# Attention in a hybrid decoder layer: the combination of a head in four later pieces, q regrouped on chip, weight loads one unit ahead of their splits

## The chip, the core and the metric

The kernel runs on one core of a Trainium2 chip. The core has a matrix engine (TensorE, PE in the profile; its weight loads are listed as PEld) and three engines for element-wise work: VectorE (DVE), ScalarE (ACT) and GpSimd (POOL). SyncE (SP) issues nearly all DMAs. Each engine takes its instructions in a fixed order; an instruction that waits holds up all that stand behind it. Matmul results lie in PSUM, all else on chip in SBUF.

The metric is the time of one execution in device microseconds: the median of several runs. A profiled execution gives a trace of every instruction; its times are for finding out where time goes.

## The reference

One decoder layer on a sequence of 2048 rows of 1024 numbers, in float32. What the change touches is the attention part: eight heads of 64 columns, and for each head three "branches", in which a query looks at keys at stride 1, 4 or 16. The branches are then combined by their softmax denominators.

```python
DILATED_BRANCHES = ((128, 1), (512, 4), (2048, 16))      # (window, dilation)

h = rms_norm(x)
z = h @ W_in                # columns: [conv u | gate B | gate C | q | k | v]
yA = B * causal_dwconv3(C * u)

def dilated_mixture(q, k, v):
    for window, dil in DILATED_BRANCHES:
        # query t attends to keys t, t - dil, t - 2*dil, ... down to t - window
        o, lse = dilated_branch(q, k, v, window, dil)     # softmax in float32
    w = softmax(stack(lses), axis=0)
    return sum(w * stack(outs), axis=0)

mix = concat(rms_norm(yA), rms_norm(yB))
x = x + mix @ W_out
x = x + swiglu(rms_norm(x))
```

## The kernel before

All products are computed in float16 with operands split into a high and a low half, so a float32 product is two or three matmuls. A weight is read as float32 ("raw"), its largest magnitude is found (L96, a maximum on VectorE, ends in the tile `vm_a`), it is scaled by a power of two and split into halves by ScalarE (a cast) and VectorE or GpSimd (a subtraction).

The kernel has these stages, one after another in PE's order.

1. Normalisation of the input and a first slice of the convolution (0 to 104 us).
2. Projections of q, k and v (104 to 368 us). There are 16 units: four pairs of heads, and for each pair four blocks of 512 rows. `project` does one unit: 192 matmuls (L1194), evictions by ScalarE (L1210), squares, a tail of small operations on VectorE and GpSimd that normalises q and k (it begins with L1214 on ScalarE and L1224 on VectorE), and the stores. v goes to DRAM as `d_v` (L1221), the halves of q and k as `d_qk` (L1243), and the halves of q once more as `d_q16` in the order of stride 16, in eight small stores (L1246). Between units the loop calls weight work. `operands` prepares the next pair's weights (in units 1, 5 and 9); `spill_conv` and `spill_out` prepare convolution and output weights and store them as halves in DRAM (in units 3, 6, 7, 8, 10, 11 and 12). Each loads its raw weights and works on them in the same call.
3. A transition, in which PE has 24 steps of convolution matmuls ("fill", 14.2 us) while the first pair's operands arrive.
4. Attention (401 to 752 us): per head 8 groups of the branch at stride 4 (b = 1), 4 at stride 16 (b = 2) and 8 at stride 1 (b = 0), so 160 groups. A group goes through a chain: s matmuls on PE (L1448), the exponential on ScalarE (L1453, tile `sm`), a mask on GpSimd (`affine_select`, L1461, one or two a group), a cast on ScalarE (L1464, `et`), the low half on VectorE (L1465), and the av matmuls on PE (L1475). The av matmuls of a group are issued three groups later; in between PE does s of later groups and about two fill steps a group (convolution and output projection).
5. The rest of the output projection and the feed-forward part (752 to 2140 us).

The operands of a pair come by `load_pair`: transposed DMA loads (L199) of q (`qT`), of k's high and low halves (`ka`, `kb`) from `d_qk`, and of `q16` from `d_q16`. They are all requested at one point, in the middle of the pair before.

The result of a group is copied from PSUM into `u` (L1480, L1483). For b = 1 and b = 2 the rows are in strided order; at the branch's end they go to DRAM as `d_u` and come back in natural order as `r` (L1492 to L1497), and the load is issued right behind the store. At the end of b = 0 `combine` is called twice, for 8 blocks of 128 rows each: two additions on GpSimd (L1400, L1401), a minimum, a maximum, a reciprocal and a scaling on VectorE (L1403 to L1406, tile `bm`), a multiplication on GpSimd (L1408) and a store (L1411). The last head does this on VectorE.

The order on each engine is set by a scheduler from the order in which the program issues instructions; `issue_after` puts an instruction behind another one.

## Time and profile before

| | |
|---|---|
| median of three runs | 2133.38 us (2132.79 to 2140.19) |
| profiled execution | 2142.32 us |
| its span, first to last instruction | 2140.6 us |
| mean granted PE clock | 0.984 |
| projections, 104 to 368.2 us | PE busy 256.9 of 264.2 |
| transition, 368.2 to 401.05 us | PE busy 14.2 of 32.85 |
| attention, 401.05 to 752 us | PE busy 324.9 of 350.95 |
| the rest, 752 to 2140.6 us | PE busy 1361.5 of 1388.6 |

PE is busy for 95% of the span. A row of a timeline gives the start, the duration, the engine, the line in the program, the operation, its output and inputs, the shapes and the count; in square brackets stands how long the engine was idle before it and what ended that. A row of waits reads: who waited for what, us in total, how often, the longest. The granted clock is the share of full speed at which PE was allowed to run.

### The profile page before, as it was taken

To read this page: it belongs to the slowest core of one execution; us is meant where nothing else is said; L and a number is where in the kernel's file an instruction comes from. 1 tells how busy PE (TensorE), PEld (TensorE's weight loads), DVE (VectorE), ACT (ScalarE), POOL (GpSimd) and SP (SyncE) were. 2 spreads that over 40 slices of the span, in tenths; PEclk is the share of its full clock that TensorE was granted. 3 is DMA by queue.
4 is the path that set the end of the run, shared out by engine and by line. 5 is a ranking of instruction groups with operands and counts; after the bars stand their busy time and mean duration, and the time that the engine had idled before them with its cause. 6 is when DMAs were issued, how large, how long until landed. Compare 5 with 4: busy or idle time off the path is not lost.

```text
span 2140.6 us, 34957 instructions
## 1 busy us (share of the span) xinstructions
PE 2027.0 (95%) x13368; PEld 1126.0 (53%) x13368; DVE 1320.6 (62%) x2483; ACT 1012.5 (47%) x1780; POOL 760.4 (36%) x809
## 2 busy tenths in 40 slices
PE   4999999698999999989999999999999999999998
PEld 2499998365566644434444444444444444444443
DVE  7454453355666877886776767676767565555454
ACT  7446566465666665553443333333433344343341
POOL 0024546355665621212221212121221246555463
PEclk9999999899999999999999999999999999999999
DMA  9568976558758477897333223322322762341432
GB/s 247 143 154 199 221 188 195 131 137 192 156 139 238 110 205 235 241 302 189 113 113 103 85 98 108 104 89 99 104 92 91 267 250 64 118 138 55 148 138 81
DMA packets 487411, 325.44 MB, mean 152 GB/s; under 512 B 274625, under 2 KB 440513, under 8 KB 485057
## 3 DMA queue, kind: packets, MB, share of 16 engines
q1 hardware_dynamic: 469552, 299.96, 50.0%
q10 hardware_dynamic: 17680, 23.16, 3.0%
q8 instruction: 106, 1.74, 0.3%
q14 instruction: 73, 0.59, 0.1%
HBM read 157.96 MB, written 121.04 MB: 130 GB/s over the span
## 4 chain that ended last, share of the span: by engine, by line
PE 65%; DMA 9%; DVE 7%; ACT 6%; SPq 5%; issue 4%; POOL 2%; DVEq 0%; ACTq 0%; POOLq 0%
PE ps L812 33%; PE ps L945 15%; SPq L199 3%; PE mm L191 3%; PE mm L192 3%; PE mm L193 3%; PE s L1448 2%; PE cvx L1194 2%; PE mm L1194 2%; PE av L1475 2%; DVE vm_a L96 1%; DMA nx_x<-in_x_dram 1%; DMA wq<-d_a 1%; DMA x<-d_x 1%; POOL sm L1461 1%
## 5 line engine op out<-in xcount | busy, mean ns | idle before, releaser
L812 PEld LDWEIGHTS <-w 128*128 128x128 f16 x3696 | 362.3, 98 | 451.5 <-issue 16.3
L812 PE MATMUL ps<-b,w 128*128 128x512 f16 x2112 | 465.9, 381 | 11.3 <-ACT s L863 5.5
L945 PE MATMUL ps<-b,w 128*128 128x512 f16 x1848 | 399.7, 379 | 2.2 <-DVE x L953 0.9
L812 PE MATMUL ps<-hb,w 128*128 128x512 f16 x1584 | 347.1, 379 | 0.0
L945 PEld LDWEIGHTS <-w 128*128 128x128 f16 x1848 | 180.8, 98 | 220.9 <-issue 3.4
L1194 PEld LDWEIGHTS <-b 128*128 128x128 f16 x3072 | 255.0, 98 | 9.1 <-issue 8.8
L705 POOL TENSOR_TENSOR t<-wq 128x512 f32<-128x512 f32 (+1 forms) x46 | 59.8, 1299 | 407.3 <-issue 230.7
L1461 POOL TENSOR_SCALAR_AFFINE_SELECT sm<-sm 128x256 f32<-128x256 f32 (+2 forms) x288 | 136.3, 495 | 143.2 <-ACT sm L1453 137.9
L1465 DVE TENSOR_TENSOR et<-sm,et 128x512 f16<-128x512 f32 (+1 forms) x160 | 121.2, 762 | 99.6 <-ACT et L1464 98.0
L818 DVE TENSOR_TENSOR s<-ps,s 128x512 f32<-128x512 f32 x220 | 150.2, 683 | 37.1 <-PE ps L812 36.6
L952 POOL TENSOR_TENSOR x<-x,s 128x512 f32<-128x512 f32 x72 | 103.0, 1432 | 170.5 <-DVE s L966 133.3
L1194 PE MATMUL cvx<-w,b 128*128 128x192 f16 x1776 | 151.2, 246 | 3.3 <-ACT f L1210 2.2
L1453 ACT ACTIVATE sm<-s,bound,kap 128x512 f32<-128x512 f32 (+1 forms) x160 | 119.1, 749 | 63.7 <-PE s L1448 33.7
L953 DVE SCALAR_TENSOR_TENSOR x<-ps,a_u,x 128x512 f32<-128x512 f32 x96 | 71.8, 749 | 100.9 <-PE ps L945 74.0
L1464 ACT CAST et<-sm 128x512 f16<-128x512 f32 (+1 forms) x160 | 93.8, 589 | 71.3 <-POOL sm L1461 70.2
L191 PE MATMUL mm<-b,wq 128*128 128x512 f16 x320 | 125.7, 393 | 0.0
L192 PE MATMUL mm<-b,wq 128*128 128x512 f16 x320 | 125.7, 393 | 0.0
L193 PE MATMUL mm<-b,wq 128*128 128x512 f16 x320 | 125.6, 392 | 0.0
L1194 PE MATMUL mm<-w,b 128*128 128x192 f16 x1296 | 113.0, 248 | 4.3 <-ACT f L1210 4.3
L722 ACT CAST w<-t 128x512 f16<-128x512 f32 x88 | 53.9, 618 | 128.7 <-PE ps L812 92.6
L1475 PE MATMUL av<-v,et 128*128 128x65 f16 x1800 | 85.4, 195 | 26.1 <-DVE et L1465 13.6
L96 DVE TENSOR_REDUCE vm_a<-wq 128x1 f32<-128x2048 f32 (+2 forms) x32 | 77.3, 2417 | 42.3 <-DMA wq<-in_w_up_dram 21.3
(288 smaller groups left out, 3215.7 us busy)
## 6 DMA issues: line engine op xcount, KB each, us to landing
d_a<-a ACTq DMA_DIRECT2D x88, 256.0 KB, 2.0
d_wd<-w SPq DMA_DIRECT2D x77, 256.0 KB, 2.0
wq<-d_a SPq DMA_DIRECT2D x64, 256.0 KB, 4.2
b<-d_wd SPq DMA_DIRECT2D x14, 1024.0 KB, 6.0
wq<-in_w_in_dram SPq DMA_DIRECT2D x24, 512.0 KB, 6.4
d_qk<-qkhl SPq DMA_DIRECT2D x16, 768.0 KB, 3.7
d_h<-hl SPq DMA_DIRECT2D x24, 512.0 KB, 3.2
wq<-in_w_gate_dram SPq DMA_DIRECT2D x22, 512.0 KB, 4.8
```

What stands on the lines that cost most here:

```text
L191: self.pe = mm(ps, lhsT=lh(k), rhs=rh(k), start=k == ks[0], stop=False)
L192: mm(ps, lhsT=lh(k), rhs=rl(k), start=False, stop=False)
L193: mm(ps, lhsT=ll(k), rhs=rh(k), start=False, stop=k == ks[-1])
L812: nc.tensor.matmul(ps[self.BANK[n]], lhsT=w[:, x, k], rhs=b[:, y, k], start=first and k == 0 and q == 0, stop=k == 3 and q == 2, skip_grou ...
L818: nc.vector.tensor_tensor(t, x, y, op=ALU.add)
L945: nc.tensor.matmul(ps[self.BANK[n]], lhsT=L[n][:, x, f], rhs=B[n][:, f, y], start=first and f == 0 and q == 0, stop=f == n_f - 1 and q == ...
L952: nc.gpsimd.tensor_tensor(o, o, s_, op=ALU.add)
L1194: self.pe = nc.tensor.matmul(ps[:, 192 * t:192 * (t + 1)], lhsT=lh(x, k), rhs=w[:, y, k], start=start and t + k + q == 0, stop=stop and k ...
L1453: nc.scalar.activation(e, sp[:, 0:o], AF.Exp, scale=self.kap, bias=self.bound)
L1461: nc.gpsimd.affine_select(m, m, pattern=pattern, compare_op=ALU.is_ge, fill=0.0, base=0, channel_multiplier=-sg)
L1465: nc.vector.tensor_tensor(et[:, 1], e, et[:, 0], op=ALU.subtract)
L1475: self.pe_av = nc.tensor.matmul(ps[:, us.index(u)], lhsT=p_, rhs=v_, start=n_ == 0, stop=n_ == len(ops) - 1)
```

## The change

1. `d_q16`, its stores and its transposed loads are gone. `regroup` makes `q16` of one head from `qT` on chip, by four copies on VectorE of 512 elements a partition, each 16 runs of 32 elements read with a step of 16. The first pair's first head is regrouped in unit 14 of the projections; in attention a pair's second head is regrouped at the pair's group 9, the next pair's first head at group 33. In the order that results, the first pair's eight copies all stand in the projections, the other 24 in attention.
2. `load_pair` is a generator. The first pair's twelve transposes are requested in units 8 to 11; of later pairs one is requested every second group. The loads of v are issued before the branch that needs them.
3. The load of `r` is issued two groups after its store. `combine` stops before its multiplication, and its four parts (additions and small operations, then multiplication and store, for each half) are called four, five, six and seven groups after the head's last output, each placed behind that group's mask.
4. `sm` has four buffers instead of three.
5. `operands`, `spill_conv` and `spill_out` are generators too: the raw loads are issued in one unit, the maximum, scaling and split in the next. The splits stand in units 1 to 10.

```diff
-        self.d_q16 = [dr.tile([S, 2 * P], F16, name=f"d_q16{g}") for g in range(4)]
...
-            for g in range(4):
-                Wg = Wn
-                for i in range(4):
-                    with ExitStack() as behind:
...
-                        if g < 3 and i == 1:
-                            Wn = self.operands(g + 1)
...
-                        k = self.SPILLS.get((g, i))
-                        if k is not None:
-                            self.spill_conv(k) if k < 3 else self.spill_out((k - 3) // 2, (k - 3) % 2)
-                    self.project(g, 3 - i if g == 3 else i, Wg)
-
-    SPILLS = {(0, 3): 0, (1, 2): 3, (1, 3): 1, (2, 0): 4, (2, 2): 5, (2, 3): 2, (3, 0): 6}
+            jobs = [None, (self.operands, 1), (self.spill_conv, 0), (self.spill_out, 0, 0), (self.spill_conv, 1),
+                    (self.operands, 2), (self.spill_out, 0, 1), (self.spill_conv, 2), (self.spill_out, 1, 0),
+                    (self.operands, 3), (self.spill_out, 1, 1)] + [None] * 6
+            job = None
+            self.st0 = {}
+            pair = self.load_pair(0, self.st0)
+            for n in range(16):
+                g, i = n // 4, n % 4
+                if i == 0:
+                    Wg = Wn
+                with ExitStack() as behind:
+                    for m in self.marks:
+                        behind.enter_context(tc.issue_after(m))
+                    if job:
+                        Wn = next(job) or Wn
+                    job = None
...
+                    if jobs[n + 1]:
+                        job = jobs[n + 1][0](*jobs[n + 1][1:])
+                        next(job)
+                    if 8 <= n < 12:
+                        for _ in islice(pair, 3):
+                            pass
+                    if n == 14:
+                        self.regroup(self.st0, 0)
+                self.project(g, 3 - i if g == 3 else i, Wg)
...
             nc.sync.dma_start(raw[:, :, m * P:(m + 1) * P], w_in[:, o:o + P].rearrange("(c p) n -> p c n", p=P))
+        yield
         s, u = self.pow2(self.wsm, self.vmax(raw.rearrange("p k c -> p (k c)")), "w", 11, 11)
...
-        for a in range(8):
-            nc.sync.dma_start(self.d_q16[g].rearrange("(r c j a) e -> c a r j e", r=NT, c=4, j=4)[c, a],
-                              hl[16 * a:16 * a + 16, :, 0:2].rearrange("p j i x d -> p j (i x d)"))
...
                 self.transpose(st[x][:, :, o], self.d_qk[g][o, 256 * i:256 * (i + 1)])
-        st["q16"] = self.q16.tile([P, 2, NT, P], F16, name="q16", bufs=2)
-        for r in range(0, NT, 4):
-            self.transpose(st["q16"][:, :, r:r + 4].rearrange("p h r a -> p h (r a)"), self.d_q16[g][P * r:P * (r + 4)])
+                yield
+
+    def regroup(self, st, h):
+        t = st["q16"][h] = self.keep.tile([P, NT, P], F16, name="q16", bufs=2)
+        for n in range(4):
+            self.nc.vector.tensor_copy(t[:, :, 32 * n:32 * n + 32],
+                                       st["qT"][:, h, 512 * n:512 * (n + 1)].rearrange("p (a r) -> p r a", r=NT))
...
+        load = self.load_pair(g + 1, nx) if g < 3 else iter(())
...
-            if (h, b) == (1, 1) and g < 3:
-                self.load_pair(g + 1, nx)
-            Vb = self.load_v(g, h, b)
+            q16, Vb = st["q16"][h], self.v_next
...
                 nc.vector.tensor_scalar_mul(bm, bm, uv)
+                if not last:
+                    yield
                 y = self.y7[:, ts] if last else X[0][:, :, 0:HD]
...
-                    e = self.ep.tile([P, 512], F32, name="sm", bufs=3)[:, 0:o]
+                    e = self.ep.tile([P, 512], F32, name="sm", bufs=4)[:, 0:o]
...
-                            t = R[h, b] = self.up.tile([P, NT, HD + 1], F32, name=f"r{b}")
-                            nc.sync.dma_start(t, du.rearrange("(b p) c -> p b c", p=P))
+
+                            def bring():
+                                t = R[h, b] = self.up.tile([P, NT, HD + 1], F32, name=f"r{b}")
+                                nc.sync.dma_start(t, du.rearrange("(b p) c -> p b c", p=P))
+                            self.todo.append((self.n + (1 if last else 2), bring))
                         elif not last:
-                            combine(0, 8)
-                            combine(8, 8)
+                            for i, step_ in enumerate(c for m in (0, 8) for c in [combine(m, 8)] * 2):
+                                self.todo.append((self.n + 4 + i, lambda step_=step_: next(step_, None)))
...
+                    for due in [t for t in self.todo if t[0] <= self.n]:
+                        self.todo.remove(due)
+                        with self.tc.issue_after(sel.ins):
+                            due[1]()
+                    if count % 2 == 0 and count > 3:
+                        next(load, None)
+                    i = 6 * g + 3 * h + (1, 2, 0).index(b) + 1
+                    if tiles.index(us) * len(us) + us.index(pr[0]) == (12 if b == 2 else 6) and i < 24:
+                        self.v_next = self.load_v(i // 6, i // 3 % 2, (1, 2, 0)[i % 3])
+                    if count == 9:
+                        self.regroup(st, 1)
+                    if count == 33 and g < 3:
+                        self.regroup(nx, 0)
                     yield self.turn
```

What this does to the order of instructions is shown at three places. The first is SP's queue at the end of the projections, before (`d_q` is `d_q16`, `q` is `q16`, `d_v` and `v` are v):

```order
L1221 DMA d_v_64<-vs_981 128x4x130 x2
L1246 DMA d_q_135<-qkhl 16x4x256 x3
L1243 DMA d_qk_139<-qkhl 128x4x768
L1246 DMA d_q_135<-qkhl 16x4x256 x5
L199 DMA_TRANSPOSE q_5266<-d_q_132 128x2x512 x4
L1372 DMA v<-d_v_61 128x2x520 x2
L1375 DMA v<-d_v_61 128x2080
L199 DMA_TRANSPOSE q_5996<-d_q_133 128x2x512 x4
L1339 DMA d_ya<-cg 128x512
```

And with the change (lines shift: L1254 stores `d_qk`, L1232 `d_v`, L1351 the convolution's result `d_ya`, L1512 `d_u`, L1519 loads `r`):

```order
L1254 DMA d_qk_135<-qkhl 128x4x768
L1232 DMA d_v_64<-vs_977 128x4x130 x2
L1254 DMA d_qk_135<-qkhl 128x4x768
L1351 DMA d_ya<-cg 128x512
L1395 DMA v<-d_v_61 128x16x130
L1512 DMA d_u_0_65<-u 32x4x260 x4
L1519 DMA r_5617<-d_u_0_65 128x16x65
```

The stores of `d_q` and the eight transposes of `q` are gone from behind the last `d_qk`; the first loads of v stand ahead of these rows.

The second place is GpSimd's order at the combination of the first pair's second head, before (selects, additions L1400 and L1401, multiplications L1408):

```order
L1461 AFFINE_SELECT sm<-sm 128x2x128 x12
L1400 TENSOR_TENSOR r_6377<-r_6377,r_6518 128x520 x2
L1461 AFFINE_SELECT sm<-sm 128x2x128 x3
L1461 AFFINE_SELECT sm<-sm 128x128
L1401 TENSOR_TENSOR u<-u,r_6377 128x520
L1461 AFFINE_SELECT sm<-sm 128x2x128
L1461 AFFINE_SELECT sm<-sm 128x128
L1461 AFFINE_SELECT sm<-sm 128x2x128
L1461 AFFINE_SELECT sm<-sm 128x128
L1401 TENSOR_TENSOR u<-u,r_6377 128x520
L1408 TENSOR_TENSOR u<-u,bm 128x8x64
```

And with the change (L1480 is the select, L1417 and L1418 the additions, L1427 the multiplication):

```order
L1480 AFFINE_SELECT sm<-sm 128x2x128 x6
L1417 TENSOR_TENSOR r_6312<-r_6312,r_6454 128x520
L1418 TENSOR_TENSOR u<-u,r_6312 128x520
L1480 AFFINE_SELECT sm<-sm 128x2x128 x2
L1480 AFFINE_SELECT sm<-sm 128x512
L1417 TENSOR_TENSOR r_6312<-r_6312,r_6454 128x520
L1427 TENSOR_TENSOR u<-u,bm 128x8x64
L1480 AFFINE_SELECT sm<-sm 128x512
L1418 TENSOR_TENSOR u<-u,r_6312 128x520
L1480 AFFINE_SELECT sm<-sm 128x512 x2
L1480 AFFINE_SELECT sm<-sm 128x2x128
L1427 TENSOR_TENSOR u<-u,bm 128x8x64
```

The same six operations stand further behind the head's end, in pairs among the selects of the next head's branches.

The third place is VectorE's order at such a combination, with the change, at the same head (L1484 is the subtraction, L1420 to L1423 the small operations, L1380 the copies of `regroup`, L1499 and L1502 the copies of av):

```order
L1484 TENSOR_TENSOR et<-sm,et 128x512
L1499 COPY u<-av 128x2x2x65
L1484 TENSOR_TENSOR et<-sm,et 128x512
L1420 TENSOR_REDUCE dmin<-u 128x1
L1421 TENSOR_SCALAR bm<-u 128x8
L1380 COPY q_6900<-qT 128x16x32 x3
L1422 RECIPROCAL bm<-bm 128x8
L1380 COPY q_6900<-qT 128x16x32
L1502 COPY u<-av 128x260
L1423 TENSOR_SCALAR bm<-bm,uv 128x8
L1484 TENSOR_TENSOR et<-sm,et 128x512 x2
```

The copies stand between the small operations of the combination, at this place and at those of the second and third pair.

36 lines of the change are left out of this document (19 added, 17 removed).

## The prediction

> **What bounds the kernel now.** I read first a table of busy time by stage. Its columns are the stretch (us from the span's start), its length, the busy time of PE, PEld, DVE, ACT and POOL with their instructions, then the granted PE clock, the share of the DMA engines and GB/s. The three rows are the projections, the transition into attention, and attention.
>
> ```profile
> 104.00:368.20 264.20, 256.93 (x3081) 255.81 (x3080) 120.68 (x257) 149.81 (x274) 117.29 (x106) 0.99 0.76 190
> 368.20:401.05 32.85, 14.20 (x66) 6.29 (x65) 7.69 (x17) 11.57 (x24) 11.91 (x14) 0.78 0.57 155
> 401.05:752.00 350.95, 324.89 (x3600) 215.54 (x3601) 224.22 (x441) 223.24 (x371) 200.44 (x341) 0.96 0.66 159
> ```
>
> PE is busy nearly throughout, so only its idle time and its slow clock can be won. It idles 32.85 - 14.20 = 18.65 us in the transition and 350.95 - 324.89 = 26.1 us in attention. Next I read PE's waits from 368.2 to 752 us (what waits, for what, us in total, times, longest).
>
> ```profile
> PE s L1448 <- DMA q<-d_q: 18.7, 1, 18.7
> PE av L1475 <- DVE et L1465: 13.6, 12, 3.0
> PE av L1475 <- ACT et L1464: 12.3, 7, 3.5
> ```
>
> And from 104 to 368.2 us:
>
> ```profile
> PE mm L1194 <- ACT f L1210: 4.3, 3, 3.1
> PE cvx L1194 <- ACT f L1210: 2.2, 2, 1.4
> ```
>
> So the idle time has three owners: one wait of 18.7 us for the transposed load of q16, 25.9 us in which the av matmuls lack exponentials, and 6.5 us in which the projections lack free PSUM. Then I asked what the stalls do to the clock (length, PE busy, clock, DMA share, GB/s).
>
> ```profile
> 308.00:312.00 4.00, 4.00 (x32) 0.57 0.91 295
> 401.05:407.00 5.95, 5.95 (x22) 0.50 1.10 236
> 444.00:453.00 9.00, 6.43 (x47) 0.81 0.32 89
> 488.00:497.00 9.00, 4.88 (x37) 0.81 0.87 198
> 531.00:541.00 10.00, 5.65 (x42) 0.83 0.16 53
> 577.00:586.00 9.00, 6.00 (x46) 0.81 1.29 189
> 619.00:624.00 5.00, 3.65 (x39) 1.00 0.29 79
> 666.00:681.00 15.00, 10.19 (x82) 0.77 0.69 196
> 704.00:717.00 13.00, 8.55 (x71) 0.87 0.29 83
> ```
>
> Length times (1 - clock) is the time lost: 1.7 us after the projections' longest stall, 3.0 after the transition, and 1.7 + 1.7 + 1.7 + 1.7 + 0 + 3.5 + 1.7 = 12.0 at the seven places in attention. The whole that this change can win is 6.5 + 1.7 + 18.65 + 3.0 + 25.9 + 12.0 = 67.75 us.
>
> **The transition.** SP's timeline at the end of the projections (start, duration, operation):
>
> ```profile
> 388.11 0.39 SPq L1243 DMA_DIRECT2D d_qk<-qkhl  x1
> 388.55 2.99 SPq L1246 DMA_DIRECT2D d_q<-qkhl  x5
> 392.88 5.27 SPq L199 DMA_TRANSPOSE q<-d_q  x4
> ```
>
> PE's first row of attention, with the idle time ahead of it:
>
> ```profile
> 401.05 0.38 PE L1448 MATMUL s<-q,ka 128*128 128x256 f16 x1 [18.65 <-DMA q<-d_q]
> ```
>
> The first instruction of a unit's tail in the last three units (shortest, median and longest ns, then first and last start), and the DMA table's row of the store that ends a tail (KB each, us to landing):
>
> ```profile
> L1214 ACT ACTIVATE row<-f x3: 1054/1058/1058, 358.8 to 378.4; 128x1024 f32<-128x1024 f32 x3
> ```
>
> ```profile
> d_qk<-qkhl SPq DMA_DIRECT2D x16, 768.0 KB, 3.7
> ```
>
> After the last unit's d_qk store, SP stores d_q, transposes it back and only then can PE start. The change removes both steps: q16 comes from qT by VectorE copies of a head whose rows were transposed earlier. What is late next is the last d_qk store itself. The first exponential's buffer lies where the projections' buffers were, so it waits until that store has landed. The store is issued at 388.11, 19.9 us after PE's end at 368.2, and takes 3.7 more: 23.6. The tail that precedes it is not long in itself: its first instruction, L1214, runs three times with (378.4 - 358.8) / 2 = 9.8 us between, less than a unit of PE (264.2 / 16 = 16.5). It is late because it begins 378.4 - 368.2 = 10.2 us behind PE's end, work left over from weight splits. Without that backlog it would begin at PE's end and the store would land about 23.6 - 10.2 = 13.4 us behind it, inside the 14.2 us of conv matmuls that PE still has. PE can besides run three groups of s, at 324.89 / 160 = 2.03 us each, before the first av is due: 14.2 + 6.1 = 20.3. The chain from exponential to av is about 3 us, an estimate from the rows in the part on attention (select 0.77, cast 0.62, subtraction 0.775, and the exponential taken like the subtraction). Bounds of the stall left: 13.4 + 3 - 20.3 is below zero, so nothing; with the backlog kept 23.6 + 3 - 20.3 = 6.3, and 1.7 of clock. I take 3, nearer to the case of a shorter backlog.
>
> **The projections.** VectorE's wait there, in the order of its queue:
>
> ```profile
> DVE vm_a L96 <- DMA t<-in_w_out_dram: 25.1, 5, 13.0
> ```
>
> VectorE stood 25.1 us on raw weights that had not landed, and everything behind it in its queue (the normalisation of q and k, the low halves of the splits) stood too; ACT, whose next work needs those, was late with the PSUM evictions L1210. The change puts the maximum one unit behind its loads, and ends the splits in unit 10 of 0 to 15 instead of 12, so five units remain, and not three, to work the backlog off. It also frees SP of 128 small stores. Bounds: the load was also issued early before, so nothing is won and 8.2 us stays; or all of it goes. I keep 2 us. The eight regroup copies of the first pair stand on VectorE just ahead of one of the last tails; at 0.7 us each (priced below) they make that tail 9.8 + 5.6 = 15.4 us, still less than a unit, and I cost them at nothing; without that cover they would be 5.6 us more at the transition.
>
> **Attention.** The stalls come once a head, at its combination. GpSimd's wait and what followed, in the timeline of all engines where R came late:
>
> ```profile
> 530.96 2.52 POOL L1400 TENSOR_TENSOR r<-r,r 128x520 f32<-128x520 f32 x2 [4.06 <-DMA r<-d_u]
> 533.43 0.77 POOL L1461 TENSOR_SCALAR_AFFINE_SELECT sm<-sm 128x256 f32<-128x256 f32 x2
> 534.17 1.28 POOL L1401 TENSOR_TENSOR u<-u,r 128x520 f32<-128x520 f32 x1
> 534.23 0.62 ACT L1464 CAST et<-sm 128x512 f16<-128x512 f32 x1 [3.20 <-POOL sm L1461]
> 534.88 1.12 DVE L1465 TENSOR_TENSOR et<-sm,et 128x512 f16<-128x512 f32 x1 [5.97 <-ACT et L1464]
> ```
>
> The head where R was there, GpSimd's row and PE's later one:
>
> ```profile
> 615.37 3.12 POOL L1400 TENSOR_TENSOR r<-r,r 128x520 f32<-128x520 f32 x2 [0.27 <-DMA r<-d_u]
> ...
> 621.08 0.42 PE L1475 MATMUL av<-v,et 128*128 128x65 f16 x8 [0.86 <-DVE et L1465]
> ```
>
> What the operations cost, GpSimd's groups from 395 to 752 us and then VectorE's (count, busy time, mean ns, idle time ahead):
>
> ```profile
> L1461 POOL TENSOR_SCALAR_AFFINE_SELECT sm<-sm 128x256 f32<-128x256 f32 x216 | 100.6, 485 | 102.2 <-ACT sm L1453 98.5 <-DVE cg L1334 2.1 <-DVE et L1465 1.4
> ...
> L1400 POOL TENSOR_TENSOR r<-r,r 128x520 f32<-128x520 f32 x14 | 18.6, 1346 | 17.7 <-DMA r<-d_u 17.7
> L1408 POOL TENSOR_TENSOR u<-u,bm 128x512 f32<-128x512 f32 x14 | 17.1, 1221 | 0.7 <-DVE bm L1406 0.7
> ```
>
> ```profile
> L1465 DVE TENSOR_TENSOR et<-sm,et 128x512 f16<-128x512 f32 x119 | 91.9, 775 | 68.1 <-ACT et L1464 66.9
> ...
> L1483 DVE COPY u<-av 128x260 f32<-128x260 f32 x62 | 26.3, 424 | 13.6 <-PE av L1475 13.0
> ```
>
> GpSimd waits 17.7 us in all for R, with selects behind it in its queue, and then adds twice in a row (2.52 us) before the next select; ACT's cast, VectorE's subtraction and PE's av follow in a chain. The change asks for the combination four to seven groups later, 4 x 2.03 = 8.1 us, against 17.7 / 7 = 2.5 us of wait a head, so the 17.7 goes. The issue of R two groups behind its d_u stores keeps SP from standing on them. What stays is GpSimd's arithmetic: four additions and two multiplications a head, 4 x 1.35 + 2 x 1.22 = 7.8 us. Over the six groups in which they now lie it also has 6 x 2 selects of 0.485 or less, 5.8: together 13.6 in 6 x 2.03 = 12.2 us. It falls behind by about 1.4 us, and by 1.35 us at each single operation, where the cover is the three groups between s and av. The head at 615 prices the case without wait: it lost little (PE's idle before 621.08 is 0.86; the clock in 619 to 624 stayed 1.00) although its two additions took 3.12 us in one lump. Bounds: nothing, or 0.86 us and a second stall like it, 1.7, at each of seven heads: 12. I take about 0.7 a head, 5 us.
>
> New on VectorE are 32 copies of 512 elements, 24 of them in attention. No row shows such a copy. The nearest below is L1483, 0.424 for 260 elements, the nearest above L1465, 0.775 for 512 with two sources; I take 0.7, so 24 x 0.7 = 17 us on an engine busy 224 of 351, and four in a row 2.8. Three heads' copies stand in the queue among the small operations of the combination; GpSimd's multiplication waits for those and selects wait behind it. Bounds 0 and 3 heads x (2.8 + 1.7 of clock) = 13.5; I keep 2.
>
> A row of this case bears on it: the subtraction beside an addition of GpSimd took 1.12 (534.88), against 0.775 on the mean. The Trainium skill, "SBUF — State Buffer", section "Who interferes with whom", says that VectorE and GpSimd share one pair of ports under an exclusive lock, which a copy between SBUF operands may take. The row agrees as far as it goes; whether these copies lock GpSimd out no trace here shows. By the lock the sum would gain up to 24 copies on GpSimd's side, and that is the second rival.
>
> **The sum.** Kept: 2 + 3 + 5 + 2 = 12 of 67.75; saved 55.75, say 56. The profiled execution took 2142.32 us with a span of 2140.6 (1.7 around it); it is 8.9 us above the median of 2133.38. The span would be 2140.6 - 56 = 2085, and the median 2133.4 - 56 = **2077 us**. Its own range, with 2 to 22 us kept: 2068 to 2088. Chance 0.57.
>
> A page speaks for a milder bill. The Trainium skill, "TensorE: Matmul & The Clock Gate", section "HAM oscillation", sets the limit for idle gaps of PE at about 3.4 us. The trace differs: the 9 us from 444 hold 2.57 us of idle time and show 0.81. By the page, stalls of 2 us left in attention would cost no clock; by the rows, 1.7 us each.
>
> **Rivals.** (1) **GpSimd stays the bound at the combination.** The arithmetic is the same 7.8 us a head. Then only the share of the wait goes, 17.7 us, and of the 25.9 + 12.0 = 37.9 half stays, 19 instead of 7: 2077 + 12 = 2089. For it: 13.6 of work in 12.2 us. Against: the head at 615. Chance 0.17. (2) **The copies hold GpSimd up**: 24 x 0.7 = 17 us, in 2077 + 17 = 2094, if each lands on a select that PE lacks. For it: the 1.12. Against: GpSimd is idle 150 of 351 us. Chance 0.08. (3) **The change doesn't do what it says in the projections**: the loads were already issued early, the splits cost the same, and the backlog stays. Then 8.2 stays instead of 2, and 8 instead of 3 at the transition: 2077 + 11 = 2088. For it: ACT has 149.81 us of work there either way. Against: the 25.1. Chance 0.11. (4) **Slower, by the copies.** Strided rows of 16 pieces could cost several times a plain copy. Six blocks of four lie in attention; each would hold the subtraction L1465, and so av, for 4c less some 2 us of cover, plus 1.7 of clock. It decides from 6 x (4c - 0.3) = 56, or c = 2.4 us, three times the upper row. At c = 3 it costs 70: 2077 + 70 = 2147. Chance 0.04. No difference, out of (1) to (3) together with c near 2: 0.03.
>
> **How the numbers follow.** What a measurement of this kernel can tell from no change is about 0.5%, 10.7 us. All of the forecast and rivals (1) to (3) lie beyond it on the faster side: 0.57 + 0.17 + 0.08 + 0.11 = 0.93; I leave 0.02 of that for sums of them that end within the bound. Faster 0.91, same 0.05, slower 0.04. Everything won gives 2133.4 - 67.75 = 2066, so the range begins at 2064; above it reaches past rival (2) to 2104.
>
> **What would show it.** Right: PE's wait for q is gone and the first s follows the fill without 18.7 us; no wait of GpSimd on r; the clock at the combinations 1.00; VectorE's wait on in_w_out under 5 us; L1380 between 0.42 and 0.78 us. Wrong: a new wait of PE on an exponential over 6 us at the start of attention (backlog), stalls of 1 to 3 us at every head with r already there (GpSimd), selects that stretch beside L1380 (ports), or copies over 2 us.

## The result and the profile after the change

| | before | with the change |
|---|---|---|
| median | 2139.72 us (13 runs, 2132.79 to 2146.36) | 2124.33 us (13 runs, 2119.21 to 2130.62) |
| span of the profiled execution | 2140.6 us | 2118.8 us |
| mean granted PE clock | 0.984 | 0.990 |

The ratio is 0.9931, with a 95% interval of 0.9916 to 0.9945: the change saves about 15 us, not 56. The three runs of before that the prediction had, with a median of 2133.38, are among the 13. The two profiled executions lie 21.8 us apart; that of before is one of the slower runs of its kernel and that of after one of the faster, so about 6 us of these are scatter. Where time went is read from the profiles all the same.

The stages of the changed kernel, cut at its own first and last matmul of each (from the span's start; length; busy time of PE, PEld, DVE, ACT, POOL; clock, DMA share, GB/s). The rows are projections, transition, attention:

```profile
104.98:370.53 265.55, 256.68 (x3082) 255.87 (x3081) 124.94 (x271) 151.51 (x282) 121.84 (x109) 0.99 0.72 184
370.53:384.61 14.08, 14.08 (x66) 6.38 (x65) 4.93 (x11) 7.78 (x16) 7.92 (x11) 1.00 0.32 110
384.61:734.61 350.00, 320.54 (x3628) 214.38 (x3627) 255.64 (x481) 224.32 (x376) 214.08 (x342) 0.98 0.61 154
```

And of before, cut in the same way:

```profile
103.83:368.16 264.33, 257.06 (x3081) 255.91 (x3081) 120.85 (x257) 149.94 (x274) 117.25 (x106) 0.99 0.76 190
368.16:401.05 32.89, 14.24 (x66) 6.29 (x65) 7.69 (x17) 11.61 (x24) 11.95 (x14) 0.78 0.57 154
401.05:754.50 353.45, 327.15 (x3626) 216.85 (x3627) 226.72 (x452) 225.09 (x376) 200.44 (x341) 0.96 0.66 160
```

The transition is as short as its fill, 18.8 us less. SP issued the last store of `d_qk` 11.9 us behind the end of the projections, and not 19.9 as before:

```profile
382.44 0.38 SPq L1254 DMA_DIRECT2D d_qk<-qkhl  x1
```

Attention is only 3.45 us shorter. What it won is clock: PE's busy time for the same matmuls fell by 6.6 us, and 3.0 of these are the slow clock behind the long wait. Its idle time has grown, from 26.3 to 29.5 us, while VectorE's busy time rose by 29 us. The projections are 1.2 us longer. PE's waits from 104 to 737 us show the new owners:

```profile
PE av L1494 <- DVE et L1484: 20.4, 17, 4.2
PE mm L1205 <- ACT f L1221: 8.2, 1, 8.2
PE av L1494 <- DVE u L1502: 5.1, 3, 2.0
...
PE av L1494 <- ACT et L1483: 0.4, 1, 0.4
```

The wait on q is gone. ScalarE's cast, which ended 12.3 us of av's waits before, ends 0.4 now; VectorE ends nearly all. And the projections have one stall of 8.2 us in place of several small ones. One of the stalls in attention, in the timeline of all engines:

```profile
528.95 0.15 DVE L1420 TENSOR_REDUCE dmin<-u 128x1 f32<-128x8 f32 x1
529.02 0.19 DVE L1421 TENSOR_SCALAR bm<-u 128x8 f32<-128x8 f32 x1
529.12 3.21 DVE L1380 COPY q<-qT 128x512 f16<-128x512 f16 x3
...
529.33 0.60 ACT L1483 CAST et<-sm 128x512 f16<-128x512 f32 x1
...
532.25 0.19 DVE L1422 RECIPROCAL bm<-bm 128x8 f32<-128x8 f32 x1
532.36 0.94 DVE L1380 COPY q<-qT 128x512 f16<-128x512 f16 x1
...
533.69 2.13 DVE L1484 TENSOR_TENSOR et<-sm,et 128x512 f16<-128x512 f32 x2
...
534.43 0.73 PE L1494 MATMUL av<-v,et 128*128 128x65 f16 x10 [4.20 <-DVE et L1484]
```

Four copies of `regroup` stand among the small operations of the combination and take 4.2 us with these; the subtraction behind them begins at 533.69, although its cast had ended at 529.93, and PE waits for it. A stall follows each of the six blocks of copies in attention, from 0.9 us at the first, the only one that stands at no combination, to this one of 4.2 us. What VectorE's operations cost, the copies first where nothing of the combination runs (in the projections), then from 384 to 737 us, then the subtraction there, and GpSimd's additions:

```profile
L1380 DVE COPY q<-qT 128x512 f16<-128x512 f16 x8 | 4.4, 617 | 0.0
```

```profile
L1380 DVE COPY q<-qT 128x512 f16<-128x512 f16 x24 | 19.5, 858 | 0.0
```

```profile
L1484 DVE TENSOR_TENSOR et<-sm,et 128x512 f16<-128x512 f32 x120 | 107.1, 900 | 48.5 <-ACT et L1483 47.3
```

```profile
L1418 POOL TENSOR_TENSOR u<-u,r 128x520 f32<-128x520 f32 x14 | 21.6, 1543 | 0.4
L1417 POOL TENSOR_TENSOR r<-r,r 128x520 f32<-128x520 f32 x14 | 20.8, 1487 | 0.0
```

A copy takes 0.617 us in the projections and 0.858 on the mean in attention; the subtraction rose from 0.775 to 0.900, the additions from 1.346 and 1.372 to 1.487 and 1.543. Nobody changed these operations. The trace shows what the longer ones have in common: of the 120 subtractions of this size, those during which GpSimd is idle take 0.69 us on the mean, and those that overlap with one of its two-input operations 1.21. Before the change 13 of them had such an overlap, with it 43. The ten copies with GpSimd idle take 0.61 us, the longest copy beside it 1.70. So the two engines hold each other up.

### The profile page after: what moved, and what is told of

It reads as the page before. It is cut to its first block, busy times and chain, and to the rows that moved or that the text cites. A ratio compares the mean times of both kernels' runs of the same rounds, so it can differ in the third digit from the quotient of the medians.

```text
span 2118.8 us, 34786 instructions
## 1 busy us (share of the span) xinstructions
PE 2019.1 (95%) x13368; PEld 1123.8 (53%) x13368; DVE 1348.2 (64%) x2515; ACT 1008.9 (48%) x1780; POOL 775.3 (37%) x809
## 4 chain that ended last, share of the span: by engine, by line
PE 65%; DVE 10%; DMA 8%; ACT 6%; issue 4%; POOL 4%; SPq 3%; DVEq 0%; ACTq 0%; POOLq 0%
PE ps L812 34%; PE ps L945 15%; PE mm L191 3%; PE mm L192 3%; PE mm L193 3%; POOL sm L1480 2%; PE cvx L1205 2%; PE s L1467 1%; PE av L1494 1%; SPq L199 1%; PE mm L1205 1%; DVE vm_a L96 1%; DMA nx_x<-in_x_dram 1%; DVE et L1484 1%; DMA b<-d_h 1%
## 5 line engine op out<-in xcount | busy, mean ns | idle before, releaser
L1480 POOL TENSOR_SCALAR_AFFINE_SELECT sm<-sm 128x256 f32<-128x256 f32 (+2 forms) x288 | 142.2, 517 | 119.9 <-ACT sm L1472 105.8
L1484 DVE TENSOR_TENSOR et<-sm,et 128x512 f16<-128x512 f32 (+1 forms) x160 | 129.3, 816 | 67.1 <-ACT et L1483 65.4
L192 PE MATMUL mm<-b,wq 128*128 128x512 f16 x320 | 122.7, 384 | 0.0
L193 PE MATMUL mm<-b,wq 128*128 128x512 f16 x320 | 122.7, 383 | 0.0
L191 PE MATMUL mm<-b,wq 128*128 128x512 f16 x320 | 122.6, 383 | 0.0
L1494 PE MATMUL av<-v,et 128*128 128x65 f16 x1800 | 86.2, 195 | 27.6 <-DVE et L1484 20.4
```

The costliest lines, as they stand in the source:

```text
L191: self.pe = mm(ps, lhsT=lh(k), rhs=rh(k), start=k == ks[0], stop=False)
L192: mm(ps, lhsT=lh(k), rhs=rl(k), start=False, stop=False)
L193: mm(ps, lhsT=ll(k), rhs=rh(k), start=False, stop=k == ks[-1])
L1480: sel = nc.gpsimd.affine_select(m, m, pattern=pattern, compare_op=ALU.is_ge, fill=0.0, base=0, channel_multiplier=-sg)
L1484: nc.vector.tensor_tensor(et[:, 1], e, et[:, 0], op=ALU.subtract)
L1494: self.pe_av = nc.tensor.matmul(ps[:, us.index(u)], lhsT=p_, rhs=v_, start=n_ == 0, stop=n_ == len(ops) - 1)
```

## The experiments

All are edits of the changed kernel, or of a kernel built from it. "Projections" and "attention" are the lengths of these stages in the run's profile, "idle" is PE's idle time in attention. The transition was 14.1 us in all of them. Each ratio is to the kernel before on the same chip.

| run | median us | ratio and interval | projections | attention | idle |
|---|---|---|---|---|---|
| the changed kernel | 2124.3 | 0.9931 (0.9916 to 0.9945) | 265.6 | 350.0 | 29.5 |
| no copies in attention | 2106.3 | 0.9864 (0.9847 to 0.9880) | 265.0 | 332.3 | 17.4 |
| one copy a group | 2113.9 | 0.9893 (0.9876 to 0.9909) | 265.4 | 339.7 | 21.6 |
| copies on ScalarE | 2120.9 | 0.9922 (0.9906 to 0.9939) | 266.5 | 345.1 | 24.6 |
| block of copies elsewhere | 2114.1 | 0.9900 (0.9870 to 0.9930) | 266.3 | 340.7 | 21.2 |
| single copies elsewhere | 2113.9 | 0.9900 (0.9870 to 0.9930) | 265.9 | 341.9 | 22.6 |
| copies, one combination | 2123.6 | 0.9957 (0.9941 to 0.9974) | 265.0 | 354.0 | 31.7 |
| no copies, one combination | 2118.1 | 0.9916 (0.9886 to 0.9947) | 266.0 | 349.9 | 28.8 |
| weight jobs at once | 2129.3 | 0.9970 (0.9957 to 0.9983) | 272.2 | 349.7 | 27.6 |
| second pair's loads later | 2121.1 | 0.9933 (0.9913 to 0.9953) | 263.0 | 348.5 | 27.3 |
| jobs in units 9, 11, 13 | 2117.8 | 0.9914 (0.9897 to 0.9931) | 257.2 | 353.4 | 30.6 |
| q16 through DRAM | 2110.5 | 0.9874 (0.9858 to 0.9891) | 269.3 | 334.9 | 16.5 |
| the same, one combination | 2132.8 | 0.9991 (0.9977 to 1.0006) | 269.2 | 360.5 | 35.3 |
| the same, three `sm` buffers | 2114.1 | 0.9889 (0.9870 to 0.9909) | 269.7 | 336.6 | 17.4 |
| the same, six pieces | 2115.6 | 0.9904 (0.9882 to 0.9925) | 271.9 | 334.9 | 17.3 |
| the same, jobs in units 9, 11, 13 | 2102.9 | 0.9854 (0.9835 to 0.9873) | 262.7 | 333.3 | 18.0 |
| all of these together | 2094.3 | 0.9807 (0.9789 to 0.9825) | 255.3 | 332.5 | 15.0 |

The stage behind attention differs as well: 1386.1 us before, 1384.2 with the change, 1387.5 without the copies, 1384 to 1392 in all of these runs. Why is not shown, but it is part of the reason that medians move less than attention.

### The copies: left out, spread, on ScalarE

Without the copies in attention:

```diff
-                    if count == 9:
+                    if count == 9 and g == 0:
                         self.regroup(st, 1)
-                    if count == 33 and g < 3:
-                        self.regroup(nx, 0)
+                    if count == 9:
+                        self.first = self.first if g else st["q16"]
+                        st["q16"][1] = self.first[1]
+                    if count == 33 and g < 3:
+                        nx["q16"][0] = self.first[0]
```

> The changed kernel without the 24 copies of regroup in attention; the heads of the second to fourth pair use the first pair's q16, so this part of the computation is left out. Theory P (the copies): the blocks of four copies on VectorE put the subtraction L1484 and the copies of av L1502 behind them late; the idle times of PE at the six blocks (408, 447, 489, 530, 576, 622 us) add up to 16.5 us, and about 5 us of clock hang on them. Then the waits of PE's av matmuls fall from 27.6 to about 11 us and the time from 2124 to about 2103. Theory C (the combination): GpSimd's additions and VectorE's subtractions hold each other up, and the copies only stand at the same place. Then the waits stay above 22 us and the time within 5 us of 2124.

Attention fell by 17.7 us to 332.3, the median to 2106.3; the theory of the copies had 2103. PE's waits in attention:

```profile
PE av L1494 <- DVE et L1484: 14.6, 16, 2.3
PE av L1494 <- DVE u L1499: 1.2, 1, 1.2
```

And the row of attention in the table by stage (columns as above):

```profile
383.28:715.58 332.30, 314.87 (x3627) 211.76 (x3625) 237.90 (x452) 223.19 (x376) 209.07 (x341) 1.00 0.64 161
```

The waits fell from 27 to 16 us, and the clock stayed at 1.00. What remains stands at the combinations. Not all of the 17.7 us belongs to the copies: in the changed kernel the clock was also lowered at 709 us, for 1.7 us, behind stalls of 1.20 and 2.33 us where no copy stands; without the copies the same stalls, 1.19 and 2.33 us, left it at 1.00. That is chance, as the last section shows, and about 16 us are left. The subtraction is as slow without the copies, so it isn't they that slow it:

```profile
L1484 DVE TENSOR_TENSOR et<-sm,et 128x512 f16<-128x512 f32 x120 | 109.6, 922 | 53.2 <-ACT et L1483 52.2
```

One copy a group:

```diff
-                    if count == 9:
-                        self.regroup(st, 1)
+                    if count in (9, 10, 11, 12):
+                        with self.tc.issue_after(sub.ins):
+                            self.regroup(st, 1, (count - 9,))
```

(and the same at groups 33 to 36; `sub` is the group's subtraction)

> The changed kernel with one copy of regroup in each of four groups, right behind the group's subtraction, and not four in one group. Theory P, if the length of the block is what hurts: single copies of 0.6 to 1.1 us fit into the slack of a group, the waits of av fall to about 12 us, the time to about 2106. Theory P, if the sum of VectorE's work beside GpSimd is what hurts: half of it, about 2115. Theory C: no change, within 5 us of 2124.

2113.9, near the 2115 of the theory that the sum of VectorE's work counts, not the 2106 of the block's length: attention fell by 10.3 of the 17.7 us. (In this run and in the two with copies "elsewhere" attention holds 28 copies and not 24, because the first pair's second head is regrouped there too.)

On ScalarE:

```diff
-                        self.regroup(st, 1)
+                        self.regroup(st, 1, self.nc.scalar.copy)
```

> The changed kernel with the copies of regroup in attention on ScalarE, four in one group as before. If VectorE and its neighbourhood with GpSimd are what hurts, the copies take about 0.6 us each whatever GpSimd does and the time falls to about 2109. If a block of four in any engine of the chain hurts, 4 x 0.6 = 2.4 us ahead of an exponential and a cast still stall PE by about 1 us at six places, and the time is about 2116. Theory C: within 5 us of 2124.

2120.9, an interval that overlaps with the changed kernel's. The size was wrong: a copy takes 1.124 us there, not 0.6, so a block is 4.5 us long.

```profile
L1380 ACT COPY q<-qT 128x512 f16<-128x512 f16 x24 | 25.4, 1124 | 0.0
```

The stalls moved from one engine of the chain to another: av now waits 8.0 us for the cast, and not 0.4.

```profile
PE av L1494 <- DVE et L1484: 12.3, 16, 2.3
PE av L1494 <- ACT et L1483: 8.0, 6, 1.9
```

### q16 through DRAM

```diff
+        if g:
+            for a in range(8):
+                nc.sync.dma_start(self.d_q16[g].rearrange("(r c j a) e -> c a r j e", r=NT, c=4, j=4)[c, a],
+                                  hl[16 * a:16 * a + 16, :, 0:2].rearrange("p j i x d -> p j (i x d)"))
...
+                    if count == 9 and g:
+                        self.load_q16(g, st, 1)
```

(`load_q16` is four transposed loads of one head; the same at group 33, and the first pair keeps its copies)

> The changed kernel with q16 of the second to fourth pair by way of DRAM again (eight stores a unit from the fifth unit on, transposed loads of one head at the groups where the copies stood); the first pair keeps its copies, which stand in the projections. Theory P: as without the copies, about 2104, since the transposed loads fall long before their use. Rival S: the 96 stores and 24 transposes stand in SP's queue ahead of d_qk, d_u and r, and cost the projections or the combinations what the copies cost: 2115 to 2124.

2110.5. Attention is 334.9, near that without copies; but the 96 stores lengthen the projections by 3.7 us, and the stall there is 11.0 us long. So both theories hold in part, and the trade is a gain of 12 us: 0.9874 against 0.9931. The kernel is complete here, so this run also confirms what the one without copies showed.

### The split of the combination

Undone with q16 through DRAM:

```diff
-                            self.todo.append((self.n + (1 if last else 2), bring))
+                            bring()
...
-                            for i, step_ in enumerate(c for m in (0, 8) for c in [combine(m, 8)] * 2):
-                                self.todo.append((self.n + 4 + i, lambda step_=step_: next(step_, None)))
+                            for m in (0, 8):
+                                for _ in combine(m, 8):
+                                    pass
```

> The kernel with q16 by way of DRAM (2110.5 us), and the combination undone: R is loaded right behind its store and the whole combination is asked for at the head's end, as before the change. If the split in four later pieces is worth what its cover was reckoned at, GpSimd waits for r again (17 us in all), the av waits rise from 15 to about 26 us with some 7 us of clock behind them, and the time is about 2128. If the split only moved the stalls, the time stays within 4 us of 2110.5.

2132.8: the split is worth 25 us there (0.9991 against 0.9874), more than was thought. GpSimd's waits say why:

```profile
POOL r L1427 <- DMA r<-d_u: 28.4, 6, 8.2
```

GpSimd waited 28.4 us for R and not 17.7 as before the change. In SP's queue the longest of these waits, 8.2 us, has an explanation: the store that R comes from stands behind q16's transposed loads, which took SP from 502 to 510 us. Without such loads the wait was 16.7 us, in the run with no copies and one combination below. Undone beside the copies, the same edit:

> The changed kernel with the copies kept and only the combination undone (R loaded right behind its store, the whole combination at the head's end). With q16 by way of DRAM the split was worth 25 us. If it is worth as much beside the copies, the split and the copies are separate terms and this kernel takes about 2148, more than before the change. If the copies had taken the split's gain back, because both fall at the same groups, it takes about 2130.

2123.6, ratio 0.9957: here the split is worth only 5.5 us. The missing corner, no copies and one combination:

> The changed kernel without the 24 copies in attention (the second to fourth pair use the first pair's q16: that part is left out) and with the combination undone. Attention took 354.0 us with copies and one combination, 350.0 with copies and four pieces, 332.3 without copies and with four pieces. If the terms are separate, 354.0 - 17.7 = 336, time about 2107. If copies and pieces cost only where they meet, the split alone is worth far more than 4 us here: attention about 350, time about 2121.

In the profiles attention takes 354.0 (copies, one combination), 350.0 (copies, four pieces), 349.9 (no copies, one combination) and 332.3 (neither). The copies cost 4.1 us beside one combination and 17.7 beside four pieces; the split earns 4.0 us with copies and 17.6 without. By the medians the same pattern is weaker: the copies cost 0.9957 - 0.9916 = 0.0041 and 0.9931 - 0.9864 = 0.0067, 9 and 14 us, the split earns 0.0026 and 0.0052, 6 and 11 us. The difference of the differences, 5.6 us, is within the four intervals together (about 9 us). That they cost more together is what the profiles show; the timed runs do not settle it.

The copies taken away from the combination, in a block and singly:

```diff
-                    if count == 9:
+                    if count == 15:
+                        with self.tc.issue_after(sub.ins):
                             self.regroup(st, 1)
```

(and at group 35; singly, one copy a group at 14 to 17 and 34 to 37)

> The changed kernel with the blocks of four copies held at the pair's groups 15 and 35, right behind the group's subtraction; in the changed kernel the order had pulled them to the groups of the combination. If meeting the combination is what makes them dear, most of the 17 us goes: attention about 335, time about 2108. If a block of four (about 2.5 us on VectorE) is too long anywhere, each still stalls PE by 1 us or more: attention 343 or more, time about 2116.

> As the run before, with one copy a group at groups 14 to 17 and 34 to 37, so that the copies neither stand in a block nor at the combination. If the meeting is the cause, about the same as the block elsewhere, 2107; if the block's length is, clearly less than that one, by 8 us. Single copies at groups 9 to 12, beside the combination, had an attention of 339.7 us.

2114.1 and 2113.9, attention 340.7 and 341.9: a block is no worse than single copies, so its length does not matter once it is away from the combination. PE's stalls behind four of the seven blocks are 0.58 to 0.91 us, behind the others under 0.4. But spread over four groups beside the combination (attention 339.7) they cost no more than here. So either remedy wins 8 to 10 of the 17.7 us in attention. In the timed runs the spread copies are clearly better than the changed kernel (0.9893 against 0.9931); at 0.9900 the intervals overlap with its own. Of the 7 to 10 us that remain, 1.7 to 3.4 are slow clock behind the stall of 1.19 and 2.33 us near 700 us, which has no copy at it, and these three runs have four copies more; the rest remains wherever the copies stand.

Six pieces, one GpSimd operation a group:

```diff
                 e.tensor_tensor(X[1], X[1], X[2], op=ALU.add)
+                if not last:
+                    yield
                 e.tensor_tensor(X[0], X[0], X[1], op=ALU.add)
...
-                            for i, step_ in enumerate(c for m in (0, 8) for c in [combine(m, 8)] * 2):
+                            for i, step_ in enumerate(c for m in (0, 8) for c in [combine(m, 8)] * 3):
```

> The kernel with q16 by way of DRAM (2110.5 us), the combination of a head in six pieces over six groups: one GpSimd operation a group. If GpSimd's two additions in a row (3 us between two masks) are what is left of the stalls at the combination, about 10 of 15 us of av waits, half of them or more go: about 2104. If additions and VectorE's subtractions hold each other up however they stand, the sum stays: within 3 us of 2110.5.

PE's waits in attention:

```profile
PE av L1506 <- DVE et L1496: 6.9, 10, 1.3
PE av L1506 <- DMA v<-d_v: 5.8, 1, 5.8
```

The mechanism was right: av's waits on the subtraction halved, from 13.7 to 6.9 us. All 160 subtractions together took as long as before, 132.6 us in both profiles, so PE had waited for GpSimd's operations in a row more than for the longer subtractions. But a load of v, behind transposed loads in SP's queue, took 5.8 back, and attention kept its length. By the ratios the kernel is 6 us slower, with intervals that overlap; the profile has 2.6 us of it in the projections (271.9 against 269.3 us, with a stall of 13.5) and 3.9 behind attention.

### The projections

Loads and split in one unit again:

```diff
                         next(job)
+                        Wn = next(job) or Wn
+                        job = None
```

> The changed kernel with each weight job's raw loads and split in one unit again (in units 0 to 9), all else as changed. If loading one unit ahead is what takes VectorE's wait for raw weights away, that wait rises again from 20.9 us and PE loses 6 us more in the projections: 2130. If the loads were hoisted by the order anyway and the 8.2 us stall at 284 us has another cause (SP late with the store of d_qk), the stall is there again and the time is within 3 us of 2124.

2129.3: loading one unit ahead is worth 8 us. VectorE's waits with the loads not ahead:

```profile
DVE vm_a L96 <- DMA t<-in_w_out_dram: 25.0, 6, 8.7
DVE vm_a L96 <- DMA wq<-in_w_in_dram: 4.4, 1, 4.4
```

In the changed kernel there is one such row, of 20.9 us, and before the change 25.1; under 5 us were forecast. PE's stalls are 8.5 and 3.3 us without and 8.2 with the loads ahead. So loading ahead helps, but the wait that it was to take away is largely still there, and the changed kernel's projections are no shorter than those of before: the jobs stand closer (units 1 to 10), and that costs as much, as the run with the jobs apart shows below.

What makes the 8.2 us stall? SP's and ScalarE's timelines in the changed kernel:

```profile
264.25 8.09 SPq L199 DMA_TRANSPOSE ka<-d_qk  x1
272.38 3.02 SPq L199 DMA_TRANSPOSE kb<-d_qk  x1
275.50 0.53 SPq L1254 DMA_DIRECT2D d_qk<-qkhl  x1
```

```profile
282.12 0.71 ACT L1250 CAST qkhl<-row 128x256 f16<-128x256 f32 x2 [12.55 <-DMA d_qk<-qkhl]
282.74 3.30 ACT L1302 ACTIVATE t<-t,w_sg 128x256 f32<-128x256 f32 x8
285.94 3.12 ACT L1145 ACTIVATE wq<-wq,w_sg 128x384 f32<-128x384 f32 x6
288.97 1.12 ACT L1251 CAST qkhl<-row 128x512 f16<-128x512 f32 x2
290.00 0.61 ACT L1145 ACTIVATE wq<-wq,w_sg 128x384 f32<-128x384 f32 x1
290.51 1.03 ACT L1303 CAST t<-t 128x1024 f16<-128x1024 f32 x1
291.45 0.61 ACT L1145 ACTIVATE wq<-wq,w_sg 128x384 f32<-128x384 f32 x1
291.96 0.56 ACT L1221 ACTIVATE f<-mm,uq 128x384 f32<-128x384 f32 x1
```

ScalarE waited 12.6 us for the tile of a store that SP had issued late; then it did the scaling of two weight jobs of neighbouring units (L1302 and L1145), and only then the eviction L1221 for which PE waited. Two edits tell the causes apart. The loads of the second pair held back (`qk_store` is the last store of `d_qk`):

```diff
-                        next(load, None)
+                        with self.tc.issue_after(self.qk_store.ins):
+                            next(load, None)
```

> The changed kernel with the second pair's twelve transposed loads held behind the last store of d_qk; in the changed kernel they stand in SP's queue in the projections. Theory T: at 264 us two of them took SP 8.1 and 3.0 us, the store of d_qk behind them was issued 10 us after its data was ready, ScalarE's cast waited 12.6 us for the tile and the evictions behind it kept PE from going on for 8.2 us. Then the stall and its slow clock go and the time falls by 8 to 10 us to about 2115. Rival: the DMA engines are loaded by the raw weights there anyway and the store lands as late: within 3 us of 2124.

No difference in time. The stall shrank to 6.0 us and the store of d_qk went out on time, at 264.70, but ScalarE's longest wait was now another:

```profile
ACT t L1302 <- DVE w_sg L1295: 7.4, 1, 7.4
```

So the late store was the nearest cause and not the one that counts. The three last jobs apart:

```diff
-                    (self.operands, 2), (self.spill_out, 0, 1), (self.spill_conv, 2), (self.spill_out, 1, 0),
-                    (self.operands, 3), (self.spill_out, 1, 1)] + [None] * 6
+                    (self.operands, 2), (self.spill_out, 0, 1), (self.spill_conv, 2), None,
+                    (self.operands, 3), None, (self.spill_out, 1, 0), None, (self.spill_out, 1, 1)] + [None] * 3
```

> The changed kernel with one edit: the last three weight jobs in units 9, 11 and 13 (the last pair's operands first, then the two halves of the output weights) and not in units 8, 9 and 10. Theory J: the 8.2 us stall of PE at 284 us is two jobs' work in one unit; ScalarE stands on the scales of both, with the evictions behind them. Then the stall and its 1.8 us of clock go, the projections fall from 265.6 to about 256 to 258 us, and the time from 2124 to about 2115. Rival T: SP's late d_qk store alone makes it; then it stays and the time is within 3 us of 2124. Rival B: the later splits make the end of the projections late, and the transition stalls by up to 9 us: no gain.

The stall fell to 1.7 us and the projections to 257.2, as the theory of two jobs in one unit had it. The store of `d_qk` was late in this run too, issued at 277.43 behind a transposed load of 7.74 us, so it is the crowding of the jobs that counts. VectorE's wait for raw weights fell to 5.3 us. The transition stayed at 14.1 us although the last split now stands in unit 13. The median fell by less, 0.9914 against 0.9931, and the intervals overlap: attention was 3.4 us longer in this profile, for which the trace names no one cause. With q16 through DRAM:

> The kernel with q16 by way of DRAM (2110.5 us; its stall in the projections is 11 us long) and the three jobs in units 9, 11 and 13. Theory J: the stall goes, 11 us and 1.8 of clock, about 2098. Otherwise within 3 us of 2110.5.

The stall went from 11.0 to 4.3 us and the projections from 269.3 to 262.7; the median fell to 2102.9, with intervals that overlap a little (0.9854 and 0.9874).

### Three buffers, and all together

The fourth buffer of `sm` taken away, with q16 through DRAM:

```diff
-                    e = self.ep.tile([P, 512], F32, name="sm", bufs=4)[:, 0:o]
+                    e = self.ep.tile([P, 512], F32, name="sm", bufs=3)[:, 0:o]
```

> The kernel with q16 by way of DRAM (2110.5 us), with three buffers of sm and not four. If the fourth buffer lets ScalarE run ahead over GpSimd's operations, the av waits rise by several us and the time to 2115 or more. If ScalarE's waits for s from PE set its pace, no difference: within 2 us.

0.9889 against 0.9874, attention 336.6 against 334.9: not told from nothing.

All that helped, in one kernel: q16 through DRAM, six pieces, the jobs apart, and the next pair's transposed loads behind the loads of v (`v_dma` is the latest of these):

```diff
-                    if count % 2 == 0 and count > 3:
-                        next(load, None)
...
+                    if count % 2 == 0 and count > 6:
+                        with self.tc.issue_after(self.v_dma.ins):
+                            next(load, None)
```

> The kernel with q16 by way of DRAM, the combination in six pieces, the jobs in units 9, 11 and 13, and the transposed loads of the next pair behind the loads of v. With six pieces the waits of av on VectorE fell from 14 to 7 us, but a load of v that stood in SP's queue behind transposed loads cost 5.8 us. If both are won and the projections' stall goes as well, about 2092. If the transposed loads only push other loads of SP back, av waits for v, r or q elsewhere and it is no better than the kernel of the run before, 2098.

2094.3 us, ratio 0.9807: 41 us faster than before and 27 faster than the change. In the projections PE is idle for 0.75 us:

```profile
101.95:357.29 255.34, 254.59 (x3081) 254.38 (x3081) 129.22 (x271) 151.78 (x279) 120.66 (x107) 1.00 0.70 190
371.37:703.92 332.55, 317.56 (x3627) 212.96 (x3626) 239.45 (x455) 224.49 (x379) 211.69 (x344) 0.99 0.78 179
```

## Why the prediction was wrong

The forecast was 2077, with a range of 2064 to 2104; measured were 2124.3. The sign held, the size did not. By the terms of its sum, in the profiles:

- **The transition** (kept 3 of 21.65): right, and better. The wait of 18.7 us and the slow clock behind it went whole; no backlog delayed the first exponential. This is nearly all that the change gained. That the way of q16 through DRAM was its cause is read from the traces, since no run puts it back for the first pair; that the splits end in unit 10 was not needed, as they end in unit 13 in the run with the jobs apart.
- **The projections** (kept 2 of 8.2): wrong. The step that failed is "The change puts the maximum one unit behind its loads, and ends the splits in unit 10 of 0 to 15 instead of 12, so five units remain, and not three, to work the backlog off." Loading ahead did help (8 us, by the run with the jobs at once), but VectorE still waited 20.9 us for raw weights, and pressing the jobs into units 1 to 10 put two of them side by side, so that ScalarE did their scaling ahead of an eviction. The stall is 8.2 us. Moving the jobs apart left 1.7 us of the stall and 5.3 of VectorE's wait. The prediction looked at VectorE's wait and counted no work of ScalarE by unit.
- **The combination** (kept 5 of 37.9): the mechanism was right, R no longer keeps GpSimd waiting, and without the copies the clock stays at 1.00. The size was off: without the copies attention has still 17.4 us of idle time, 12 more than forecast. The step is "I take about 0.7 a head, 5 us", read from a head where R was there and PE's idle time was 0.86 us. In the new order two or three of GpSimd's operations still stand in a row between two masks, at each of the seven heads, and 43 of 120 subtractions overlap with its operations instead of 13. One GpSimd operation a group halved av's waits on the subtraction; what makes up the other half is not shown.
- **The copies** (kept 2 in attention): the largest miss, 17.7 us in the profiles (about 16 without the chance of the clock) and 14 by the medians. The price of one alone was right, 0.62 against the 0.7 taken; the step that failed is "Three heads' copies stand in the queue among the small operations of the combination", with the bounds 0 and 13.5, of which 2 were kept. All six blocks stalled PE, and five of them stood at a combination, not three. (VectorE's order shown ahead of the prediction is, in the trace, that of the first pair's first head, at 444 to 450 us; at the second head, from 487 us, the copies stand there as well.) A copy in attention takes 0.86 on the mean, the subtraction behind a block comes late, and the two longest stalls cost the clock too. The value was taken at the low end of the bounds though the order showed the meeting.

Of the signs that would show it right, PE's wait for q is gone and GpSimd never waits for r; the clock at the combinations (0.55 from 531 to 538 us, 0.79 from 576 to 584), VectorE's wait for raw weights and the copies' 0.858 us came out against it.

The three faster rivals each had the size of one term nearly right, but not each its reason. (1) had 19 us stay at the combination instead of 7, and 17.4 stayed without the copies, though not as a backlog of GpSimd alone. (2) had the copies cost 17, in 17.7, by holding GpSimd up; GpSimd did wait 7.5 us for the scaling on VectorE (1.1 without the copies), but PE's waits end with the late subtraction on VectorE, so that the number fits is partly luck. (3) had 11 us more in the projections and the transition; the projections alone brought 8.9 of idle time and the clock behind the stall, from the crowding of the jobs, while its ground, that loading ahead does nothing, was false, and so was its loss at the transition. The error was to treat them as alternatives, each with its small chance: they act in different places and came together. Their sum, 2077 + 12 + 17 + 11 = 2117, is near the 2124 measured, which after the above is partly luck too; the range ended at 2104.

The rule of the Trainium skill ("SBUF — State Buffer", section "Who interferes with whom") fits what was measured: the copy is 0.61 us with GpSimd idle and up to 1.70 beside it, and two-input subtractions and additions slow each other. No run here shows the port itself.

## What to carry to other kernels

Work that is moved off a queue lands on an engine: look up in the order which instructions it will stand between, and price it there, not by the engine's busy share. Before moving a job to an earlier stage, add up each engine's work by unit, since a job less in one unit is a job more in another. Where two edits of one change make use of the same slack, time them apart and together.

## What the runs showed of the hardware

A strided copy of 512 float16 elements took 0.617 us on VectorE and 1.124 on ScalarE, so ScalarE was no relief. One transposed load held SP's queue for 8.1 us, where its like from 282 us on took 1.2 to 1.3 each; raw weights were being loaded beside it, and all DMAs together moved 263 GB/s from 264 to 272 us:

```profile
264.00:272.00 8.00, 3.95 (x8) 1.00 1.10 263
```

(length, ScalarE's busy time, clock, DMA share, GB/s.) That the load was slow because of them is an inference. 

The clock follows a grid of fixed steps. In each of the eighteen traces of this case, all stretches of lowered clock begin whole multiples of 3.41 us apart, and in them the clock is halved, so that one step costs 1.7 us. PE's idle time in the step before decides. From 100 us on, taking the steps at full clock: none of the 4003 with less than 1.7 us of idle time was followed by half the clock, all 116 with more than 2.05 us were, and of the 52 between 11 were. Steps of this grid (length, PE busy, clock, DMA share, GB/s), first with the change:

```profile
446.43:449.84 3.41, 1.45 (x11) 1.00 0.59 141
449.84:453.25 3.41, 2.84 (x37) 1.00 0.05 13
705.84:709.25 3.41, 0.29 (x4) 1.00 0.90 190
709.25:712.66 3.41, 3.01 (x16) 0.50 0.98 235
```

And before, where the prediction read its price of 1.7 us:

```profile
444.54:447.95 3.41, 0.84 (x16) 1.00 0.00 0
447.95:451.36 3.41, 3.41 (x20) 0.50 0.65 194
```

Before, stalls of 1.92 and 0.65 us fell into one step, 2.57 us of idle time, and the next step ran at half the clock. With the change, stalls of 2.02 and 0.51 us were cut by a boundary, 1.96 and 0.57 us, and cost nothing. From 706 to 709 us one step held 3.1 us of idle time; without the copies a boundary cut the same stalls into 1.7 and 1.8 us. Where the grid lies against a stall is chance, so the prediction's 1.7 us for a stall of 2 us is one of two outcomes. The limit of about 3.4 us for idle gaps that the Trainium skill gives ("TensorE: Matmul & The Clock Gate", section "HAM oscillation") does not hold here: at five of the six places in attention where the clock was lowered before the change, the longest gap was 1.9 to 3.3 us, and the measurement decides.
